# A two-layer decoder trunk on one core: turning the input of the next stage at the end of an FFN, and low halves of weights by an adding DMA

## The chip, the cores and the metric

The kernel runs on one core of one Trainium2 chip. The metric is the device time of one launch in microseconds (us); the time before is the median of three runs. TensorE (PE) multiplies, PEld is its weight load, VectorE (DVE) and ScalarE (ACT) work elementwise, GpSimd (POOL) here issues adding DMAs, and SyncE (SP) issues the plain DMAs. The profile comes from one further execution; times inside it count from its first instruction.

## What is computed

Two layers, each with three sub-layers on x, which is 512 tokens by 1024 features in float32:

```python
for l in range(DEPTH):
    h = rms_norm(x, gn[0])
    x = x + 0.5 * rms_norm(swiglu(h, w_ffn1_gate[l], w_ffn1_up[l], w_ffn1_down[l]), gn[1])
    h = rms_norm(x, gn[2])
    ...                                   # HGRN2 recurrence and windowed attention, gated, then w_out
    x = x + rms_norm(mixed @ w_out[l], gn[3])
    h = rms_norm(x, gn[4])
    x = x + 0.5 * rms_norm(swiglu(h, w_ffn2_gate[l], w_ffn2_up[l], w_ffn2_down[l]), gn[5])
```

`swiglu(h, g, u, d)` is `(silu(h @ g) * (h @ u)) @ d`, with an inner width of 2816. So there are four FFNs and two mixers, and each begins with a norm of the x that the one before it leaves.

## The kernel before

**Split products.** Every large matrix is multiplied in a reduced float type, float32r, and each operand is split into a high half (a cast) and a low half (the operand minus its high half). A product is three matmuls, `mm3` (line 408): high by high, then high by the other operand's low half, then low by high. PE runs its instructions in the order in which the code gives them (`manual_schedule`, line 52). The order on the other engines is the scheduler's, except for instructions passed to `pin`, which keep the order of the code among themselves.

**The stream of weights.** `Stream` (line 155) holds all weights in the order in which PE uses them, as units of 128x1024 elements. `load` (line 234) brings a unit into one of four buffers `w32` by a DMA on SP's queue; where a unit must be put together from four pieces it is four DMAs (line 240). A buffer is reused when all readers of the earlier unit are done. `split` (line 321) makes the halves `whi` and `wlo`, of which there are six each (`WS`); `ahead` (line 369) lets it run three units (`AHEAD`) before the unit that PE uses. ACT makes the high half by a cast (line 352). The low half depends on the unit's kind: kind "u" subtracts the high half from the weight on DVE (line 359); for the kinds "v", "a" and "d" ACT writes minus the weight into the float32r tile of the low half, which rounds it to minus the high half (line 356), and an adding DMA that POOL issues (line 357) adds the float32 weight to it. Either way the low half is first read by the second matmul of `mm3`.

**The end of an FFN.** `down` (line 688) multiplies by the last matrix; `y[t][h]` is the sum for token tile t (four of 128 tokens) and half h of the features (512 each). In an FFN (`fast`) 16 of the 22 blocks of the inner width go through seven products of a Strassen scheme (`quarters`, line 904). The last six blocks, three units per half h, are multiplied straight: those of h=0 first (`both`, line 729), those of h=1 last (`piece`, line 710). On PE the end is: product 5, the pieces of t=0 and t=1 with the three units of h=1, product 4 for t=2 and t=3, the pieces of t=2, then `pre.turn(0, ...)`, then the pieces of t=3, then the next stage's first products (`quad`, line 948).

**The norms there.** `half` (line 814) adds a sum to its Strassen part on DVE (line 820), squares it on ACT with a sum (`squares`, line 624, pinned) and multiplies by the gain on DVE (line 823). `post(t)` (line 836) takes the root (`root`, line 629: DVE, ACT's square root, pinned, and DVE's reciprocal) and adds the result to x (line 841). `norm(t)` (line 845) squares the new x, takes a root and scales it (line 852) into `xn[t]`, the next stage's normalized input with tokens on the partitions.

**The turn.** `Pre.turn` (line 599) turns `xn` to features on the partitions for half of the tokens (half 0: t=0 and 1). PE transposes four feature blocks at a time (line 124, from line 607), 16 transposes in all, into four PSUM banks; each bank is emptied into the high half by two ACT instructions (line 612, pinned) and into the low half by two on DVE (line 618). There are five banks of tag `acc` and three of tag `aux`. The second half (t=2 and 3) is turned by `rest` (line 867), which PE's order places a fixed count of work after the next stage has begun. The next stage's `quad` goes over the first half of the tokens with four units of weights, and then over the second half with the same units. While the first pass of `quad` runs, `ws.pinned` pins the casts of the weights; it is also set from product 6 until `half(1, 1)`.

Behind the last FFN there is no next stage, so nothing is turned. Behind a mixer (`fast` false) the turn stands at another place, which the change leaves as it was.

Of the kernel before, what the change touches and what calls it, by code (L numbers as in the profile page):

```python
# [7 lines left out]
F32 = mybir.dt.float32  # L8
F32R = mybir.dt.float32r
# [35 lines left out]
def trunk(ctx: ExitStack, tc: tile.TileContext, xin, wall, gains, lbT, hgain, sinks, c_dist, c_mask, c_ident, out):  # L45
# [109 lines left out]
    class Stream:  # L155
# [38 lines left out]
        def rows(self, kt, fast):  # L194

            u0 = self.wall

            def pieces(j, h):  # L200
                b = [(4 * h + i) * kt + 2 * j for i in range(4)]
                return [(slice(i * 2 * P, (i + 1) * 2 * P), wall[u0 + n // 8][:, n % 8 * P : (n % 8 + 2) * P]) for i, n in enumerate(b)]

            def unit(j, h):
                c = 2 * j * P
                self.src[self.n] = [(None, wall[u0 + 4 * h : u0 + 4 * h + 4, :, c : c + 2 * P].rearrange("u p c -> p u c"))] if kt == 8 else pieces(j, h)
                self.plain(1)

            lead = range(SEVEN // 2 if fast else 0, kt // 2)
            for j in lead:  # L210
                unit(j, 0)
            if fast:

                u, n = self.n, SEVEN // 4
                for q in range(n):
                    self.src[u + q] = pieces(q, 0)
                    self.src[u + n + q] = pieces(n + q, 0)
                self.side.append(([pieces(n + q, 1) for q in range(n)], [pieces(q, 1) for q in range(n)]))
                def product(k):
                    for q in range(n):  # L220
                        it = Item(k, u, 4)
                        it.q, it.n = q, n
                        self.items.append(it)

                for k in ORDER:
                    product(k)
                self.n += 2 * n
            for j in lead:
                unit(j, 1)
            if fast:  # L230
                product("p4")
            self.wall = u0 + kt
# [88 lines left out]
        def split(self):  # L321
            it = self.items[self.done]
            if it.kind[0] == "p":
                return self.quarter(it)
            u, last = it.u, it.kind in "uvd"
            self.load(u + (1 if it.kind in "uv" else 2))
            it.hi = sb.tile([P, D], F32R, tag="whi", name=nm("whi"), bufs=WS)
            it.lo = sb.tile([P, D], F32R, tag="wlo", name=nm("wlo"), bufs=WS)
            w, h = self.raw[u], (slice(0, D // 2), slice(D // 2, D))
            cols = (slice(0, D),)  # L330
            if it.kind == "u" and u == 0:
                cols = h
            if it.kind in "bcd":
                v = self.raw[u + 1]
            if it.kind == "b":

                self.t13 = sb.tile([P, D], F32, tag="tt", name=nm("tt"), bufs=2)
                pin(nc.vector.tensor_tensor(self.t13[:, h[0]], w[:, h[0]], v[:, h[0]], op=ALU.add))
                pin(nc.vector.tensor_tensor(self.t13[:, h[1]], v[:, h[0]], v[:, h[1]], op=ALU.add))
                w = self.t13  # L340
                self.product()
            elif it.kind == "c":

                t = sb.tile([P, D], F32, tag="tt", name=nm("tt"), bufs=2)
                pin(nc.vector.tensor_tensor(t[:, h[0]], self.t13[:, h[0]], v[:, h[1]], op=ALU.add))
                pin(nc.vector.tensor_tensor(t[:, h[1]], t[:, h[0]], w[:, h[1]], op=ALU.add))  # L346
                w = t
            elif it.kind == "d":
                w = v
                cols = h[1:]  # L350
            for c in cols:
                i = nc.scalar.copy(it.hi[:, c], w[:, c])  # L352
                if u < 3 or self.pinned or self.tight:
                    pin(i)
                if it.kind in "vad":
                    self.hold(nc.scalar.mul(it.lo[:, c], w[:, c], -1.0))  # L356
                    nc.gpsimd.dma_start(it.lo[:, c].bitcast(F32), w[:, c], accum_op=ALU.add)  # L357
                else:
                    self.hold(nc.vector.tensor_tensor(it.lo[:, c], w[:, c], it.hi[:, c].bitcast(F32), op=ALU.subtract))  # L359
            self.done += 1  # L360
            self.flight += 1
            if last:
                nu = u + (1 if it.kind in "uv" else 2)
                for i in range(u, nu):
                    self.raw.pop(i)
                    self.freed += 1
                self.load(self.freed + W32)
# [207 lines left out]
    class Pre(Quarters):  # L575
# [20 lines left out]
        def raw(self, half, i):  # L596
            return [cut(self.h[k + 4 * i], HALF[half]) for k in range(4)]

        def turn(self, half, get):

            c = HALF[half]
            for kp in range(KT // 2):
                p = get(kp)
                for i in range(2):
                    for t in range(2):
                        k = 2 * kp + i
                        transpose(p[:, (2 * i + t) * P : (2 * i + t + 1) * P], self.xn[2 * half + t][k // 4][:, k % 4 * P : (k % 4 + 1) * P])
                for i in range(2):
                    k = 2 * kp + i
                    if half == 0:  # L610
                        self.h.append((big(F32R), big(F32R)))
                    pin(nc.scalar.activation(
                        out=self.h[k][0][:, c], in_=p[:, i * 256 : (i + 1) * 256], func=AF.Copy,
                        scale=g_sb[:, self.l, self.n, k : k + 1],
                    ))
                for i in range(2):
                    k = 2 * kp + i
                    nc.vector.scalar_tensor_tensor(
                        self.h[k][1][:, c], p[:, i * 256 : (i + 1) * 256], g_sb[:, self.l, self.n, k : k + 1],
                        self.h[k][0][:, c].bitcast(F32), op0=ALU.mult, op1=ALU.subtract,  # L620
                    )
                self.have[half] += 2

    def squares(v, o):

# [62 lines left out]
    def down(src, kt, l, n, nxt, fast):  # L688
# [145 lines left out]
            left[0] -= 1  # L834

        def post(t):
            if not fast or t != 1:
                half(t, 1)
            rc = root(ss[t], D)
            for h in range(2):  # L840
# [34 lines left out]
        for t in range(TT):  # L875
# [5 lines left out]
            for j, b in zip(last, bs):  # L881
# [1 line left out]
                    piece(b, t, 1, j, i)  # L883
                    order.poll()
                ws.used(b)
                if pre and (t, j) == ((2, last[-1]) if fast else (3, last[TURN])):
                    pre.turn(0, lambda kp: acc() if kp < 3 else aux())
                    if not fast:
                        norm(2)
            if not fast or t > 1:  # L890
                post(t)
                after(t)
            elif t == 0:
                post(0)
            else:
                half(1, 1)
                ws.pinned = False
# [531 lines left out]
    for l in range(DEPTH):  # L1429
        for n in (0, 2, 4):  # L1430
            if n == 2:
                ws.plain(2 * H + 6 + 8 + LATE * 3 // 2)
                for _ in range(KT - LATE // 2):
                    ws.gates()
                ws.rows(KT, False)
            else:
                p = FIRST if l + n == 0 else 3
                ws.plain(min(2 * p, 8))
                ws.plain(max(2 * p - 8, 0), "v")
                ws.pairs(FT - p)  # L1440
                ws.rows(FT, True)
# [155 lines left out]
```

## Time and profile before

| | |
|---|---|
| median of 3 runs | 2089.57 us (2086.2 to 2092.58) |
| the profiled execution | 2090.36 us |
| its span, first to last instruction | 2088.6 us |
| PE busy in the span | 2071.2 us, 99% |
| PEld busy | 1862.1 us, 89% |
| DVE busy | 1645.3 us, 79% |
| ACT busy | 1242.3 us, 59% |
| POOL busy | 257.2 us, 12% |

The page of the profile lists busy times, the time in 40 slices, the DMA queues and the costliest groups. The view of waits says which instruction sat idle on its engine and which other instruction released it: "DVE rt L634 <- ACT rt L633: 11.2, 16, 0.8" says that line 634 on DVE waited for line 633 on ACT, 11.2 us in all, 16 times, 0.8 us at most. A row of the timeline is the start, the duration, engine, line, operation, output<-input, the shape and the count, and in brackets the idle time before it with its releaser. A matmul's duration there is its latency; the distance between two starts is what it costs PE.

### The profile page before, as it was taken

The page shows a single profiled execution, that of the slowest core. Times are in us where ns is not written, and L with a number is a line of the kernel's source. Part 1 is how long each engine was busy: PE and PEld are TensorE (multiplying, and loading weights), DVE is VectorE, ACT ScalarE, POOL GpSimd, SP SyncE. Part 2 cuts the span into 40 slices and gives each one's busy share as a digit, 9 for nine tenths or more (in the row PEclk, how much of TensorE's full clock was granted, in tenths as well). Part 3 has the DMA queues.
Part 4 walks back from the last instruction along what each step waited for, and adds up shares of the span by engine and source line. Part 5 has one row for each costly group of instructions (what it writes and reads, how often), then busy time and mean ns, then how long its engine had stood idle before and what let it go on. Part 6 is the DMA issues. An engine that isn't in the chain of part 4 may idle for free.

```text
span 2088.6 us, 36534 instructions
## 1 busy us (share of the span) xinstructions
PE 2071.2 (99%) x13561; PEld 1862.1 (89%) x13561; DVE 1645.3 (79%) x2921; ACT 1242.3 (59%) x2194; POOL 257.2 (12%) x306
## 2 busy tenths in 40 slices
PE   9999999999999999999999999999999999999998
PEld 7899988887898999998899999888778989999986
DVE  5887889766776778878988878987677758787888
ACT  6556686456354556558756566854653545665684
POOL 0111140000000011113101111300000000111140
PEclk9999999999999999999999999999999999999999
DMA  8587795312246368779737877943122552777694
GB/s 246 151 186 186 173 204 193 112 61 71 72 98 206 112 152 187 186 179 207 196 103 186 188 186 190 198 168 102 51 81 61 136 188 92 187 185 183 174 207 121
DMA packets 165074, 321.78 MB, mean 154 GB/s; under 512 B 18880, under 2 KB 84896, under 8 KB 164896
## 3 DMA queue, kind: packets, MB, share of 16 engines
q1 hardware_dynamic: 122416, 228.16, 32.8%
q0 software_dynamic: 42336, 91.24, 26.4%
q8 instruction: 106, 1.74, 0.3%
q14 instruction: 72, 0.59, 0.1%
q10 hardware_dynamic: 144, 0.05, 0.0%
HBM read 213.43 MB, written 14.73 MB: 109 GB/s over the span
## 4 chain that ended last, share of the span: by engine, by line
PE 87%; ACT 4%; DVE 3%; DMA 3%; issue 2%; SPq 1%; DVEq 0%; ACTq 0%
PE acc L114 64%; PE aux L114 21%; DMA w<-wall 1%; PE aux L124 1%; DVE s L260 1%; ACT whi L285 1%; ACT s L438 1%; DMA s<-wall 1%; PE acc L124 1%; ACT s L439 1%; DVE wlo L293 1%; SPq L240 1%; DVE s L429 0%; DMA s<-xin 0%; ACT s L428 0%
## 5 line engine op out<-in xcount | busy, mean ns | idle before, releaser
L114 PE MATMUL acc<-s,whi 128*128 128x256 f32 (+1 forms) x4976 | 1053.3, 309 | 1.4 <-ACT whi L352 0.8
L114 PEld LDWEIGHTS acc<-s,whi 128*128 128x128 f32 x4976 | 809.7, 191 | 49.2 <-issue 3.2
L114 PE MATMUL acc<-s,wlo 128*128 128x256 f32 (+1 forms) x2488 | 765.2, 308 | 0.1
L114 PEld LDWEIGHTS acc<-s,wlo 128*128 128x128 f32 x2488 | 475.6, 191 | 23.3 <-DVE wlo L359 0.4
L114 PE MATMUL acc<-whi,s 128*128 128x512 f32 x1360 | 441.7, 393 | 0.0
L352 ACT CAST whi<-w 128x1024 fp32r<-128x1024 f32 (+1 forms) x309 | 287.1, 933 | 168.0 <-PE acc L114 90.8
L352 ACT CAST whi<-tt 128x1024 fp32r<-128x1024 f32 x160 | 167.6, 1048 | 255.8 <-DVE tt L346 195.1
L114 PEld LDWEIGHTS acc<-whi,s 128*128 128x128 f32 x1360 | 255.3, 188 | 57.5 <-ACT whi L352 1.6
L359 DVE TENSOR_TENSOR wlo<-tt,whi 128x1024 fp32r<-128x1024 f32 x160 | 196.1, 1226 | 137.0 <-ACT whi L352 134.7
L357 POOL DMA_DIRECT2D wlo<-w x166 | 143.3, 863 | 1200.1 <-DVE wlo L359 504.6
L114 PE MATMUL acc<-wlo,s 128*128 128x512 f32 x680 | 265.1, 390 | 0.0
L114 PE MATMUL aux<-s,whi 128*128 128x256 f32 (+1 forms) x1296 | 239.2, 285 | 0.0
L359 DVE TENSOR_TENSOR wlo<-w,whi 128x1024 fp32r<-128x1024 f32 (+1 forms) x143 | 172.0, 1214 | 81.6 <-ACT whi L352 79.7
L114 PEld LDWEIGHTS aux<-s,whi 128*128 128x128 f32 x1296 | 202.7, 192 | 1.1 <-issue 0.5
L114 PE MATMUL aux<-s,wlo 128*128 128x256 f32 (+1 forms) x648 | 184.3, 284 | 0.0
L114 PEld LDWEIGHTS acc<-wlo,s 128*128 128x128 f32 x680 | 127.8, 188 | 25.4 <-DVE wlo L293 0.4
L114 PE MATMUL aux<-whi,s 128*128 128x512 f32 x432 | 143.7, 390 | 0.0
L356 ACT ACTIVATE wlo<-w 128x1024 fp32r<-128x1024 f32 (+1 forms) x166 | 140.7, 848 | 0.0
L440 POOL DMA_DIRECT2D s<-s x128 | 111.2, 945 | 218.5 <-ACT s L428 97.3
L114 PEld LDWEIGHTS aux<-s,wlo 128*128 128x128 f32 x648 | 124.4, 192 | 0.3
L293 DVE TENSOR_TENSOR wlo<-s,whi 128x512 fp32r<-128x512 f32 x160 | 102.7, 685 | 9.9 <-ACT whi L285 9.9
L428 ACT CAST s<-s 128x512 fp32r<-128x512 f32 (+1 forms) x140 | 70.7, 547 | 44.8 <-DVE s L487 41.4
(181 smaller groups left out, 2481.7 us busy)
## 6 DMA issues: line engine op xcount, KB each, us to landing
w<-wall SPq DMA_DIRECT2D x267, 512.0 KB, 3.8
wlo<-w POOLq DMA_DIRECT2D x86, 512.0 KB, 5.3
w<-wall SPq DMA_DIRECT2D x224, 128.0 KB, 3.5
wlo<-w POOLq DMA_DIRECT2D x80, 256.0 KB, 3.4
s<-wall SPq DMA_DIRECT2D x128, 128.0 KB, 3.9
s<-s POOLq DMA_DIRECT2D x64, 256.0 KB, 4.4
x_d<-s SPq DMA_DIRECT2D x48, 256.0 KB, 2.0
s<-x_d SPq DMA_DIRECT2D x48, 256.0 KB, 4.7
```

The costliest lines, as they stand in the source:

```text
L114: nc.tensor.matmul(o, lhsT, rhs, start=start, stop=stop)
L124: nc.tensor.transpose(o, src, ident)
L240: nc.sync.dma_start(w.rearrange("p (m c) -> p m c", m=4) if c is None else w[:, c], a)
L260: pin(nc.vector.tensor_tensor(o[c], x[c], y[c], op=op))
L285: i = nc.scalar.copy(it.hi[:, h[c]], w[c])
L293: pin(nc.vector.tensor_tensor(it.lo[:, h[c]], w[c], it.hi[:, h[c]].bitcast(F32), op=ALU.subtract))
L352: i = nc.scalar.copy(it.hi[:, c], w[:, c])
L356: self.hold(nc.scalar.mul(it.lo[:, c], w[:, c], -1.0))
L357: nc.gpsimd.dma_start(it.lo[:, c].bitcast(F32), w[:, c], accum_op=ALU.add)
L359: self.hold(nc.vector.tensor_tensor(it.lo[:, c], w[:, c], it.hi[:, c].bitcast(F32), op=ALU.subtract))
L428: (hold or ws.hold)(nc.scalar.copy(hi, src))
L440: nc.gpsimd.dma_start(lo.bitcast(F32), src, accum_op=ALU.add)
```

## The change

It has two parts.

**The turn.** `turn` gets an argument `later`, and the emptying of a bank moves into a method `leave`. Behind an FFN with a next stage, the 16 transposes stand at the same place of PE's order, but one bank is of tag `acc` and three of `aux` (before: three `acc` and one `aux`), and the emptying of the four banks is written between the steps of the norms: bank 0 between `half(2, 1)` and `post(2)`, bank 1 between `post(2)` and `norm(2)`, then, behind the pieces of t=3, bank 2 between `post(3)` and `norm(3)`, and bank 3 after `norm(3)`. Before, all four stood ahead of `half(2, 1)`.

**Low halves by an adding DMA.** Units of kind "u" become kind "v": the three units of h=1 at the end of each of the four FFNs (line 229), and the four units of the `quad` that follows an FFN (both mixers, and the first FFN of layer 1). The ACT instruction of line 356 is pinned where the cast ahead of it is pinned by `ws.pinned`; before, only where `ws.tight` was set.

```diff
--- before.py
+++ after.py
@@ -201,10 +201,10 @@
                 b = [(4 * h + i) * kt + 2 * j for i in range(4)]
                 return [(slice(i * 2 * P, (i + 1) * 2 * P), wall[u0 + n // 8][:, n % 8 * P : (n % 8 + 2) * P]) for i, n in enumerate(b)]
 
-            def unit(j, h):
+            def unit(j, h, kind="u"):
                 c = 2 * j * P
                 self.src[self.n] = [(None, wall[u0 + 4 * h : u0 + 4 * h + 4, :, c : c + 2 * P].rearrange("u p c -> p u c"))] if kt == 8 else pieces(j, h)
-                self.plain(1)
+                self.plain(1, kind)
 
             lead = range(SEVEN // 2 if fast else 0, kt // 2)
             for j in lead:
@@ -226,7 +226,7 @@
                     product(k)
                 self.n += 2 * n
             for j in lead:
-                unit(j, 1)
+                unit(j, 1, "v" if fast else "u")
             if fast:
                 product("p4")
             self.wall = u0 + kt
@@ -353,7 +353,9 @@
                 if u < 3 or self.pinned or self.tight:
                     pin(i)
                 if it.kind in "vad":
-                    self.hold(nc.scalar.mul(it.lo[:, c], w[:, c], -1.0))
+                    i = nc.scalar.mul(it.lo[:, c], w[:, c], -1.0)
+                    if self.pinned or self.tight:
+                        pin(i)
                     nc.gpsimd.dma_start(it.lo[:, c].bitcast(F32), w[:, c], accum_op=ALU.add)
                 else:
                     self.hold(nc.vector.tensor_tensor(it.lo[:, c], w[:, c], it.hi[:, c].bitcast(F32), op=ALU.subtract))
@@ -596,30 +598,38 @@
         def raw(self, half, i):
             return [cut(self.h[k + 4 * i], HALF[half]) for k in range(4)]
 
-        def turn(self, half, get):
-
-            c = HALF[half]
+        def turn(self, half, get, later=False):
+
+            outs = []
             for kp in range(KT // 2):
                 p = get(kp)
                 for i in range(2):
                     for t in range(2):
                         k = 2 * kp + i
                         transpose(p[:, (2 * i + t) * P : (2 * i + t + 1) * P], self.xn[2 * half + t][k // 4][:, k % 4 * P : (k % 4 + 1) * P])
-                for i in range(2):
-                    k = 2 * kp + i
-                    if half == 0:
-                        self.h.append((big(F32R), big(F32R)))
-                    pin(nc.scalar.activation(
-                        out=self.h[k][0][:, c], in_=p[:, i * 256 : (i + 1) * 256], func=AF.Copy,
-                        scale=g_sb[:, self.l, self.n, k : k + 1],
-                    ))
-                for i in range(2):
-                    k = 2 * kp + i
-                    nc.vector.scalar_tensor_tensor(
-                        self.h[k][1][:, c], p[:, i * 256 : (i + 1) * 256], g_sb[:, self.l, self.n, k : k + 1],
-                        self.h[k][0][:, c].bitcast(F32), op0=ALU.mult, op1=ALU.subtract,
-                    )
-                self.have[half] += 2
+                outs.append(lambda kp=kp, p=p: self.leave(half, kp, p))
+                if not later:
+                    outs.pop()()
+            return outs
+
+        def leave(self, half, kp, p):
+
+            c = HALF[half]
+            for i in range(2):
+                k = 2 * kp + i
+                if half == 0:
+                    self.h.append((big(F32R), big(F32R)))
+                pin(nc.scalar.activation(
+                    out=self.h[k][0][:, c], in_=p[:, i * 256 : (i + 1) * 256], func=AF.Copy,
+                    scale=g_sb[:, self.l, self.n, k : k + 1],
+                ))
+            for i in range(2):
+                k = 2 * kp + i
+                nc.vector.scalar_tensor_tensor(
+                    self.h[k][1][:, c], p[:, i * 256 : (i + 1) * 256], g_sb[:, self.l, self.n, k : k + 1],
+                    self.h[k][0][:, c].bitcast(F32), op0=ALU.mult, op1=ALU.subtract,
+                )
+            self.have[half] += 2
 
     def squares(v, o):
 
@@ -834,7 +844,7 @@
             left[0] -= 1
 
         def post(t):
-            if not fast or t != 1:
+            if not fast or t > 1 and not pre:
                 half(t, 1)
             rc = root(ss[t], D)
             for h in range(2):
@@ -883,14 +893,27 @@
                     piece(b, t, 1, j, i)
                     order.poll()
                 ws.used(b)
-                if pre and (t, j) == ((2, last[-1]) if fast else (3, last[TURN])):
+                if pre and not fast and (t, j) == (3, last[TURN]):
                     pre.turn(0, lambda kp: acc() if kp < 3 else aux())
-                    if not fast:
-                        norm(2)
-            if not fast or t > 1:
+                    norm(2)
+            if pre and fast and t == 2:
+                outs = pre.turn(0, lambda kp: aux() if kp else acc(), True)
+                half(2, 1)
+                outs[0]()
+                post(2)
+                outs[1]()
+                norm(2)
+            elif pre and fast and t == 3:
+                half(3, 1)
+                post(3)
+                outs[2]()
+                norm(3)
+                outs[3]()
+            elif not fast or t > 1:
                 post(t)
                 after(t)
             elif t == 0:
+                half(0, 1)
                 post(0)
             else:
                 half(1, 1)
@@ -1429,13 +1452,15 @@
     for l in range(DEPTH):
         for n in (0, 2, 4):
             if n == 2:
-                ws.plain(2 * H + 6 + 8 + LATE * 3 // 2)
+                ws.plain(4, "v")
+                ws.plain(2 * H + 2 + 8 + LATE * 3 // 2)
                 for _ in range(KT - LATE // 2):
                     ws.gates()
                 ws.rows(KT, False)
             else:
                 p = FIRST if l + n == 0 else 3
-                ws.plain(min(2 * p, 8))
+                ws.plain(4, "v" if l and not n else "u")
+                ws.plain(min(2 * p, 8) - 4)
                 ws.plain(max(2 * p - 8, 0), "v")
                 ws.pairs(FT - p)
                 ws.rows(FT, True)
```

## The prediction, written before the result was known

> **What bounds the kernel now.** I read the page first, then PE's waits, then the timeline around each wait.
>
> ```profile
> PE 2071.2 (99%) x13561; PEld 1862.1 (89%) x13561; DVE 1645.3 (79%) x2921; ACT 1242.3 (59%) x2194; POOL 257.2 (12%) x306
> ```
>
> PE is busy for 99% of the span, so what can be won is what PE still waits for, and any new wait of PE is paid in full. PE's waits, the longest first (total, times, longest):
>
> ```profile
> PE acc L124 <- DVE s L852: 5.7, 3, 1.9
> PE acc L124 <- DVE s L841: 2.6, 1, 2.6
> PE aux L114 <- DVE wlo L359: 2.5, 4, 1.1
> ```
>
> Two of the three lie where the change works. The first is the second turn behind the three FFNs that have a next stage: PE's transposes wait for `xn[3]`, the last result of `norm(3)`. The third comes four times, once in each FFN: the first low half of the units for h=1 at t=0. The second is at the very end of the kernel, where nothing is turned, and stays. So the change can win at most 5.7 + 2.5 = 8.2 us.
>
> **The turn.** PE behind the first FFN (the next stage's first product, then the second turn), then ACT and DVE there:
>
> ```profile
> 353.16 0.40 PE L114 MATMUL acc<-s,whi 128*128 128x256 f32 x2
> ```
>
> ```profile
> 362.04 0.27 PE L124 MATMUL acc<-ident,s 128*128 128x128 f32 x1
> 364.20 0.55 PE L124 MATMUL acc<-ident,s 128*128 128x128 f32 x3 [1.90 <-DVE s L852]
> ```
>
> ```profile
> 349.56 0.82 ACT L612 ACTIVATE s<-acc,g_sb 128x256 fp32r<-128x256 f32 x2
> ```
>
> ```profile
> 353.03 0.85 ACT L612 ACTIVATE s<-aux,g_sb 128x256 fp32r<-128x256 f32 x2
> 353.74 0.66 ACT L627 ACTIVATE s<-s 128x512 f32<-128x512 f32 x1
> ```
>
> ```profile
> 348.81 0.68 DVE L820 TENSOR_TENSOR s<-acc,s 128x512 f32<-128x512 f32 x1
> ```
>
> ```profile
> 353.65 0.68 DVE L820 TENSOR_TENSOR s<-acc,s 128x512 f32<-128x512 f32 x1
> ```
>
> ```profile
> 360.93 1.42 DVE L841 SCALAR_TENSOR_TENSOR s<-s,rt,s 128x512 f32<-128x512 f32 x2
> ```
>
> ```profile
> 363.66 0.88 DVE L852 TENSOR_SCALAR s<-s,rt 128x512 f32<-128x512 f32 x2
> ```
>
> `half(2, 1)` has its sum at 348.81 + 0.68 = 349.5, but its square runs at 353.74: it is pinned behind the eight evictions of line 612. Everything of t=2 and then of t=3 is late by these 4.2 us. The change lets two evictions (0.82) stand between that square and the root, and two more (0.85) ahead of `norm(2)`. I follow the longer of the two remaining chains, that of t=3, from its sum at 353.65, which PE sets: the sum 0.68, a square with its read 0.9, a root with its reciprocal and handovers 0.6, so line 841 starts at about 355.8 instead of 360.93. From line 841 to line 852 it is 363.66 - 360.93 = 2.7; bank 2's two evictions may come between, 0.85. That puts line 852 at 359.4 and its first result at 359.9, 2.1 before PE comes for it at 362.04. The norm of t=2 is done by then: it no longer waits for four banks. Bank 1 must be empty when the next stage reads its features: it starts at 353.16, and each bank feeds 24 matmuls of 256 columns, at half of the 0.227 us that 512 take (below) 2.7 us, so bank 1 is wanted at 355.9, banks 2 and 3 at 358.6 and 361.3; by the chain above they are empty at about 353, 357 and 360, in time by 3, 2 and 1. PE's order, the place of the second turn and the count of transposes stay as they were, and the third `aux` bank, which held `y[3][0]`, is read at 348.2 by line 820, earlier still once DVE has less to do. I put the turn's win at the whole 5.7 us, three times 1.9. If the cover fails (the margin of 2.1 is used up), at most the 5.7 stay.
>
> **Low halves at the end of the FFN.** These three units per FFN come just in time already. ACT's casts of all three behind the first FFN (I call the FFNs A, B, C, D) and of the first unit in the others:
>
> ```profile
> 317.00 1.05 ACT L352 CAST whi<-w 128x1024 fp32r<-128x1024 f32 x1 [0.99 <-DMA w<-wall]
> 319.00 1.05 ACT L352 CAST whi<-w 128x1024 fp32r<-128x1024 f32 x1 [0.95 <-DMA w<-wall]
> 321.64 1.05 ACT L352 CAST whi<-w 128x1024 fp32r<-128x1024 f32 x1 [1.60 <-DMA w<-wall]
> ```
>
> ```profile
> 1007.28 1.06 ACT L352 CAST whi<-w 128x1024 fp32r<-128x1024 f32 x1 [0.58 <-DMA w<-wall]
> ```
>
> ```profile
> 1351.86 1.06 ACT L352 CAST whi<-w 128x1024 fp32r<-128x1024 f32 x1 [0.80 <-issue]
> ```
>
> ```profile
> 2042.53 1.05 ACT L352 CAST whi<-w 128x1024 fp32r<-128x1024 f32 x1 [0.65 <-DMA w<-wall]
> ```
>
> The casts wait for the weights themselves, so they don't move earlier. PE's wait in the four places, and DVE's subtractions in A:
>
> ```profile
> 324.07 0.50 PE L114 MATMUL aux<-wlo,s 128*128 128x512 f32 x1 [0.58 <-DVE wlo L359]
> ```
>
> ```profile
> 1014.77 0.50 PE L114 MATMUL aux<-wlo,s 128*128 128x512 f32 x1 [0.34 <-DVE wlo L359]
> ```
>
> ```profile
> 1359.12 0.50 PE L114 MATMUL aux<-wlo,s 128*128 128x512 f32 x1 [1.12 <-DVE wlo L359]
> ```
>
> ```profile
> 2049.94 0.50 PE L114 MATMUL aux<-wlo,s 128*128 128x512 f32 x1 [0.47 <-DVE wlo L359]
> ```
>
> ```profile
> 322.80 3.49 DVE L359 TENSOR_TENSOR wlo<-w,whi 128x1024 fp32r<-128x1024 f32 x3
> ```
>
> Without the wait PE wants the first low half at 323.49 (A), 1014.43 (B), 1358.00 (C) and 2049.47 (D). DVE was busy until 322.80, so the cast of 317.00 lay there for 4.7 us. The change takes 3.5 us off DVE in each FFN and ends this wait; in its place comes the path over ACT, POOL and the DMA. One such path as the kernel has it elsewhere, and the sizes and times to landing of all of them:
>
> ```profile
> 1063.95 1.05 ACT L352 CAST whi<-w 128x1024 fp32r<-128x1024 f32 x1 [5.05 <-PE acc L114]
> ```
>
> ```profile
> 1066.26 0.86 POOL L357 DMA_DIRECT2D wlo<-w  x1 [62.28 <-ACT wlo L356]
> ```
>
> ```profile
> DMA to landing us min/median/max: 4.6/4.6/4.6
> ```
>
> ```profile
> wlo<-w POOLq DMA_DIRECT2D x86, 512.0 KB, 5.3
> ```
>
> ```profile
> wlo<-w POOLq DMA_DIRECT2D x80, 256.0 KB, 3.4
> ```
>
> From the cast's start to POOL's issue it is 1066.26 - 1063.95 = 2.3 us, and 4.6 more to landing with nothing alongside. With loads alongside it is longer; two windows from an add's issue to its landing show it (first the plain queue's packets, MB and share of the window, then the add with its time to landing), then the share of the DMA engines in the four microseconds from the issue in A and in D, before the change, as the last number but one:
>
> ```profile
> q1 hardware_dynamic: 571, 0.59, 31.6%
> ```
>
> ```profile
> wlo<-w POOLq DMA_DIRECT2D x1, 512.0 KB, 6.0
> ```
>
> ```profile
> q1 hardware_dynamic: 403, 0.98, 43.5%
> ```
>
> ```profile
> wlo<-w POOLq DMA_DIRECT2D x1, 512.0 KB, 8.0
> ```
>
> ```profile
> 319.30:323.30 4.00, 4.00 (x19) 3.15 (x17) 4.00 (x7) 2.40 (x4) 0.00 (x0) 1.00 0.71 223
> ```
>
> ```profile
> 2044.83:2048.83 4.00, 4.00 (x19) 3.33 (x18) 4.00 (x8) 3.13 (x5) 0.00 (x0) 1.00 0.87 276
> ```
>
> The plain queue had 31.6% of 6.0 = 1.9 us of work beside the first add and 43.5% of 8.0 = 3.5 us beside the second. In A there are 0.71 x 4 = 2.8 us of loads (the third unit's weights, and x for the norms), so I take 4.6 + (8.0 - 4.6) / 3.5 x 2.8 = 7.3 as the upper and 4.6 + (6.0 - 4.6) / 1.9 x 2.8 = 6.7 as the lower estimate, and use 6.7 for A and, as an estimate from its likeness, for B and C. D has 0.87 x 4 = 3.5: 8.0. The first low half then lands at cast + 2.3 + this:
>
> A 317.00 + 2.3 + 6.7 = 326.0, 2.5 late. B 1016.3, 1.9 late. C 1360.9, 2.9 late. D 2052.8, 3.3 late. Sum 10.6.
>
> The next two adds follow in the same queue. Two adds of 512 KB issued 1.9 us apart:
>
> ```profile
> L357 POOL DMA_DIRECT2D wlo<-w x2: 865/934/1004, 32.9 to 34.8; - x2
> ```
>
> ```profile
> DMA to landing us min/median/max: 7.0/7.3/7.6
> ```
>
> They land at 39.9 and 42.4, 2.5 apart. PE uses up a unit at t=0 in six matmuls of 0.227 (18 whole ones in 4 us, row above), 1.36 us. So the second and the third unit are each 2.5 - 1.36 = 1.14 later still: 2.3 per FFN, 9.1 in all. New waits 10.6 + 9.1 = 19.7; the old 2.5 goes. **This part costs 17.2 us.** From t=1 on all six halves are there.
>
> What else moves: the buffers `w32` come free at the add's landing instead of after the subtraction, so SP's next load, and five loads of x queued behind it, go out some 2 us later; the casts of the next units wait for a free `whi` until 337.78 in A, and PE is later too: nothing. ACT gets 1.0 us for each of 24 units, in gaps: its 59% leaves them.
>
> **Low halves in the next stage's first pass.** Four units, three times. DVE loses four subtractions of 1.2 us around the turn, which is spare already once the turn waits for nothing. Behind A the first and the fourth are cast here:
>
> ```profile
> 337.78 1.06 ACT L352 CAST whi<-w 128x1024 fp32r<-128x1024 f32 x1 [0.46 <-PE aux L114]
> ```
>
> ```profile
> 350.64 1.05 ACT L352 CAST whi<-w 128x1024 fp32r<-128x1024 f32 x1 [0.26 <-PE acc L114]
> ```
>
> The first three have 9 us and more until they are used, one after another 2.7 apart from 353.16 on. The fourth waits for a free tile and is wanted at 353.16 + 8.2 = 361.3; 350.64 + 2.3 + 8.0 is 360.9 even with loads alongside, so nothing, and up to 2 us each, 6 in all, if ACT's pinned evictions push the negation back by that much. Below nothing there is no room: PE doesn't wait there now.
>
> **The sum.** -5.7 + 17.2 = +11.5 on the profiled execution's 2090.36: 2101.9. That execution lies 0.8 above the median of the runs, so 2101.1; I say 2101.
>
> The Trainium skill ("DMA: Bandwidth & Descriptors", section on the anatomy of one DMA on the SWDGE path) fits such a transfer's time as 2.0 us plus bytes over 436e3; for 512 KB that would be 3.2 us, an estimate by that page, with which the first low halves are in time and the sum is about -6. The add above took 4.6 with nothing alongside, so the trace doesn't agree.
>
> **The rivals.**
>
> *The adds land in time* (not slower). If an add took 3.4 us, as the 256 KB ones do, A's first low half would land at 322.7, ahead of 323.49, and its third at 327.3 against 326.2: at most 1.1 late. With 0 to 4.4 us for the four together instead of 2.5, and the turn's 5.7, that is 2081 to 2086. It decides at 4.2, 4.9, 3.8 and 4.6 us to landing (wanted time less issue in A to D); for it speaks that DVE's backlog is real, against it that the add that ran alone, at 4.6, is at that border and loads run alongside. 10%.
>
> *The adds run as if alone.* At 4.6 to landing the first are 0.4, 0, 0.8 and 0 late, with 9.1 for the queue 10.3: -2.5 - 5.7 + 10.3 = +2.1, 2092. At the median of 5.3 it is +4.6, 2094. 24%.
>
> *The turn keeps a wait* (the change doesn't do what it says): the adds as forecast, and the 5.7 not won or a late fourth unit of up to 6 in its place: 2107. 8%.
>
> *The forecast*, adds slowed by loads: 2096 to 2105 (8.0 us to landing in all four gives 14.5 for the first halves, -5.7 - 2.5 + 14.5 + 9.1 = +15.4). 58%.
>
> **How the numbers follow.** Eight in ten: the forecast, the adds alone and the turn that keeps a wait hold 90%; the range is 2089 to 2110 (the adds at 8.0 and the turn's 5.7 not won give 2110) and leaves out the adds in time and the edges. About 0.3%, 6.3 us, is what a measurement of this kernel can tell from no change. Faster by more needs the adds in time nearly everywhere: 0.08. Within it are the adds alone and the rest of those in time: 0.27. Slower: 0.65.
>
> **What would show it.** Right: PE's wait for line 852 is gone; "PE aux L114 <- DVE wlo L359" is replaced by a wait for the DMA `wlo<-w`, with three steps in each FFN, the first 2 to 3 us, the next about 1. The squares of `half(2, 1)` come straight after its sum. Wrong: adds of 512 KB at the end of the FFN that land within 4.5 us, or in less than 2.5 us of each other; line 852 still late at the second turn; waits in the next stage's first pass.

## The result, and the profile after

The changed kernel takes 2112.44 us (median of 6 runs, 2108.54 to 2114.1) where the kernel before, beside it on the same chip, took 2090.69. The ratio is 1.0101, with a 95% interval of 1.0085 to 1.0117: slower by 21 us, in the forecast direction but 2 us beyond the end of the forecast range. The profiled execution took 2113.47 us, its span is 2111.7. Engines first, as for the kernel before:

```profile
PE 2083.1 (99%) x13561; PEld 1868.5 (88%) x13561; DVE 1621.3 (77%) x2897; ACT 1263.1 (60%) x2218; POOL 277.2 (13%) x330
```

PE is "busy" for 99% again, of a span 23 us longer, with the same 13561 matmuls. The waits of PE after (total, times, longest):

```profile
PE aux L114 <- DMA wlo<-w: 19.5, 12, 5.0
PE acc L124 <- DVE s L851: 2.6, 1, 2.6
PE aux L114 <- DVE eps_t L137: 1.1, 1, 1.1
PE acc L114 <- ACT whi L352: 0.8, 1, 0.8
```

Line 852 (862 in the changed file) is gone from the list. In place of the 2.5 us for VectorE's low half stand 19.5 us for the DMA, twelve times, three per FFN. That is nearly the 19.7 us of the prediction, but by luck: the four first waits are 3.23, 3.23, 4.96 and 3.18 us, 14.6 where 10.6 was forecast, and the eight others 4.9 where 9.1 was forecast, because PE, itself slowed, came late to them. And the total is far off all the same: the list of waits doesn't hold the rest. It is in how fast PE works between these waits. PE at the end of FFN A, the units of h=1 at t=0 (start, duration, wait in brackets):

```profile
326.43 0.79 PE L114 MATMUL aux<-wlo,s 128*128 128x512 f32 x1 [3.23 <-DMA wlo<-w]
327.02 1.05 PE L114 MATMUL aux<-whi,s 128*128 128x512 f32 x2
...
330.73 0.79 PE L114 MATMUL aux<-wlo,s 128*128 128x512 f32 x1 [1.37 <-DMA wlo<-w]
...
333.91 0.80 PE L114 MATMUL aux<-wlo,s 128*128 128x512 f32 x1 [0.26 <-DMA wlo<-w]
...
336.47 0.63 PE L114 MATMUL aux<-whi,s 128*128 128x512 f32 x2
```

Two matmuls take 1.05 us from 327.02 on and 0.63 from 336.47 on. The same stretch by windows (PE, PEld, DVE, ACT, POOL busy; granted clock; DMA share; GB/s):

```profile
318.68:322.09 3.41, 3.41 (x16) 2.83 (x16) 3.41 (x7) 3.31 (x5) 1.72 (x2) 1.00 0.97 256
322.09:325.51 3.42, 1.11 (x5) 0.57 (x4) 3.42 (x7) 3.39 (x6) 0.86 (x1) 1.00 1.04 254
325.51:328.92 3.41, 2.49 (x6) 1.82 (x6) 3.02 (x6) 3.28 (x8) 0.00 (x0) 0.50 1.10 283
328.92:332.33 3.41, 2.04 (x6) 1.32 (x5) 0.00 (x0) 0.00 (x0) 0.00 (x0) 0.50 1.05 237
332.33:335.75 3.42, 3.16 (x8) 2.01 (x7) 0.00 (x0) 0.00 (x0) 0.00 (x0) 0.50 1.03 394
335.75:339.16 3.41, 3.41 (x16) 2.81 (x15) 2.95 (x5) 0.72 (x2) 0.00 (x0) 1.00 0.86 350
```

Two things are to be seen. The granted clock is 0.50 for three windows after one in which PE had 1.11 us of work; at the four FFNs' ends together it is 0.50 for 41 us. And the DMA engines are busy without a gap, a share of 0.97 to 1.10, for as long as the adds are under way. What they carried: SP's issues before and after, in the same place (an "x5" is five loads in a row).

```profile
318.06 1.35 SPq L727 DMA_DIRECT2D s<-x_d  x3
324.05 0.33 SPq L243 DMA_DIRECT2D w<-wall  x1
324.48 2.55 SPq L727 DMA_DIRECT2D s<-x_d  x5
```

```profile
318.35 5.34 SPq L737 DMA_DIRECT2D s<-x_d  x7
326.44 0.33 SPq L243 DMA_DIRECT2D w<-wall  x1
326.87 1.41 SPq L737 DMA_DIRECT2D s<-x_d  x1
```

Before, the next load of weights stood between the third and the fourth load of x and held five of them back until its buffer was free. After, that load stands behind the seventh, so seven of the eight loads of x go out beside the first adds. In FFN B and C it is the same; behind D no weights follow, and the eight loads of x go out in one row before and after. From issue to landing the three adds took, in FFN A, B, C and D:

```profile
DMA to landing us min/median/max: 7.3/9.6/10.7
DMA to landing us min/median/max: 8.6/9.3/9.8
DMA to landing us min/median/max: 8.0/9.5/11.2
DMA to landing us min/median/max: 8.6/9.1/9.6
```

I add up the stage "pieces of t=0 and t=1" (36 matmuls from the first `aux<-whi` to the next product): before 9.04, 8.79, 9.59 and 8.96 us in A to D, together 36.4; after 17.30, 16.80, 20.09 and 15.77, together 70.0. That is +33.6, of which 17.0 are waits (19.5 less 2.5) and 16.6 are matmuls at half clock. The turns and what lies around them give some 10 back (8.1 of it between the first turn's start and the second's end, in three places): +23.1 between the two profiled executions.

### The profile page after: what moved, and what is told of

The parts are those of the page before. It is cut to its first block, busy times and chain, and to the rows that moved or that the text cites. A ratio compares the mean times of both kernels' runs of the same rounds, so it can differ in the third digit from the quotient of the medians.

```text
span 2111.7 us, 36595 instructions
## 1 busy us (share of the span) xinstructions
PE 2083.1 (99%) x13561; PEld 1868.5 (88%) x13561; DVE 1621.3 (77%) x2897; ACT 1263.1 (60%) x2218; POOL 277.2 (13%) x330
## 5 line engine op out<-in xcount | busy, mean ns | idle before, releaser
L114 PEld LDWEIGHTS acc<-s,wlo 128*128 128x128 f32 x2488 | 475.1, 191 | 23.1 <-DVE wlo L361 0.4
L359 POOL DMA_DIRECT2D wlo<-w x190 | 163.6, 861 | 1292.1 <-DVE wlo L361 502.1
L361 DVE TENSOR_TENSOR wlo<-w,whi 128x1024 fp32r<-128x1024 f32 (+1 forms) x119 | 143.3, 1213 | 81.4 <-ACT whi L352 79.6
L356 ACT ACTIVATE wlo<-w 128x1024 fp32r<-128x1024 f32 (+1 forms) x190 | 165.7, 873 | 0.0
L114 PE MATMUL aux<-whi,s 128*128 128x512 f32 x432 | 153.2, 414 | 0.0
L293 DVE TENSOR_TENSOR wlo<-s,whi 128x512 fp32r<-128x512 f32 x160 | 102.6, 685 | 12.5 <-ACT whi L285 12.4
L114 PE MATMUL aux<-wlo,s 128*128 128x512 f32 x216 | 91.7, 425 | 19.5 <-DMA wlo<-w 19.5
```

The lines of the kernel that those rows point to most:

```text
L114: nc.tensor.matmul(o, lhsT, rhs, start=start, stop=stop)
L293: pin(nc.vector.tensor_tensor(it.lo[:, h[c]], w[c], it.hi[:, h[c]].bitcast(F32), op=ALU.subtract))
L356: i = nc.scalar.mul(it.lo[:, c], w[:, c], -1.0)
```

## The experiments

The theory after the result has three parts: the adds cost what they cost with little beside them (the prediction's 17); the loads of x that now run beside them make them land later; and PE's waits bring half clock behind them. The rivals: the adds are slow by their own queue whatever runs beside them, and half clock alone is the overrun.

**The turn without any new add.** Each `"v"` of the change is a `"u"` again:

```
-                unit(j, 1, "v" if fast else "u")
+                unit(j, 1)
...
-                ws.plain(4, "v")
+                ws.plain(4, "u")
...
-                ws.plain(4, "v" if l and not n else "u")
+                ws.plain(4, "u")
```

> The changed kernel with every low half subtracted by VectorE again, so that only the new order of the turn is left. My theory now: the turn is worth more than the 5.7 us of the prediction, because in the changed kernel the distance between the two turns fell and the 3.41 us of half clock behind the old wait at 1056 are gone too: 8 to 10 us less than before, 2080 to 2083. The prediction's figure would give 2085. Rival: the turn only gained in the changed kernel because the adding DMAs took four subtractions from VectorE there; then the wait for the root's scaling (L862) comes back in part and the gain is under 4 us, 2087 or more. The waits for a low half before t=0 are again four steps of VectorE with about 2.5 us in all.

Measured: 2084.44 us, ratio 0.9962 [0.9948, 0.9975], so 7.9 us less than before; the interval, 5 to 11, holds the prediction's 5.7 as well as my 8 to 10. By the trace the three turns won 1.7, 2.1 and 1.7 us (from the first turn's start to the second's end, 18.68 to 16.96 in A): the prediction's 5.7 nearly to the digit. Of the rest of the first expectation the trace shows one piece: the half clock behind FFN B's old wait is gone, and the 50 matmuls behind that turn take 5.98 us instead of 7.12. That the turn is worth 8 to 10 us isn't shown. One small wait is left in this kernel, at the first turn:

```profile
350.21 0.66 PE L124 MATMUL aux<-ident,s 128*128 128x128 f32 x4 [0.17 <-DVE s L830]
```

**The turn and the adds of the next stage's first pass.** Only the first of the three edits above:

> The changed kernel with VectorE's subtraction for the last three units of each FFN only; the new turn and the adding DMAs of the next stage's first pass are kept. My theory, as in the prediction: these adds cost nothing, so within 1.5 us of the turn alone, 2079 to 2084. Rival one: they cost up to 6 us (late fourth unit), 2087. Rival two: they relieve VectorE at the turn and gain 2 us or more, under 2079.

Measured: 2081.13 us, ratio 0.9950 [0.9938, 0.9962], 10.4 us less than before and the fastest kernel here. The step from the turn alone, 2.5 us, lies inside the intervals, but the trace has its place: the first turn's matmuls run through without the wait above, and the two turns start 14.47 us apart, not 15.32, behind each of three FFNs (3 x 0.85 = 2.6).

```profile
348.17 0.60 PE L124 MATMUL acc<-ident,s 128*128 128x128 f32 x4
348.61 1.47 PE L124 MATMUL aux<-ident,s 128*128 128x128 f32 x12
```

VectorE starts to empty the third `aux` bank (line 830) at 345.49 here and at 349.47 with the turn alone, 4 us later. So by the trace the four subtractions that the adds take over were not spare there, and rival two of the expectation has the right size, though its figure (under 2079) was missed and the step in the runs is not clear of noise.

**The adds at the FFN's end alone.** The kernel before with these lines:

```
-            def unit(j, h):
+            def unit(j, h, kind="u"):
...
-                self.plain(1)
+                self.plain(1, kind)
...
-                unit(j, 1)
+                unit(j, 1, "v" if fast else "u")
...
-                    self.hold(nc.scalar.mul(it.lo[:, c], w[:, c], -1.0))
+                    i = nc.scalar.mul(it.lo[:, c], w[:, c], -1.0)
+                    if self.pinned or self.tight:
+                        pin(i)
```

> The kernel before with the adding DMAs for the last three units of each FFN alone; old turn, low halves of the next stage's first pass by VectorE. My theory: the whole loss is here, some 31 to 35 us, 2121 to 2126: 17 of waits for the DMA and the rest of half clock behind them. The prediction's figure is 17.2 us, 2108. Rival: the adds of the next stage's first pass have part of the loss; then less than 28 us, under 2118.

Measured: 2114.38 us, ratio 1.0110 [1.0096, 1.0124]: +23 us. That is less than my 31 and more than the prediction's 17, in the range of the rival; but the rival's reason is not the one, since the pass's adds won time in the run above. The loss is here, and it is 9 us smaller than the step from the turn and the pass (0.9950) to the whole change (1.0101), which is 32 us. Its waits say half of why (line 854 is the old line 852):

```profile
PE aux L114 <- DMA wlo<-w: 22.8, 11, 4.7
PE acc L124 <- DVE s L854: 1.3, 3, 0.4
```

The old turn's wait is 1.3 us instead of 5.7 without any change of the turn. VectorE has three subtractions less and PE comes later, so the norms are nearly in time. The other half is at the FFNs' ends: the four stages take 66.5 us in all, 3.5 less than in the changed kernel, and the clock there is at 0.50 for 20 us, not 41. The gain of the new turn and the loss of the adds don't add up: beside these adds the turn is worth little.

**Zeros in the waits.** PE is kept busy ahead of the three units at t=0:

```
             for j, b in zip(last, bs):
+                if fast and t == 0:
+                    for _ in range(14 if j == last[0] else 8):
+                        nc.tensor.matmul(y[0][1], zt[0], halves(b[2], 0), start=False, stop=False)
                 for i in range(2):
                     piece(b, t, 1, j, i)
...
+        zt.append(const([P, P], "zt", F32R))
+        nc.scalar.mul(zt[0], ones, 0.0)
```

> The changed kernel with 14, 8 and 8 useless matmuls of a zero matrix, added to one bank of the sum, ahead of the three units at t=0, so that PE is busy while the adds land; the sum is unchanged, the work is added and of no use. If idling is what halves the clock behind these waits, the windows at 0.5 there are gone. Theory A, the third landing sets the end of the pieces anyway and half clock mostly lies beside the waits: 4 to 6 us less than the changed kernel, 2106 to 2109. Theory B, half clock is paid in full on top of the waits: 11 to 16 us less, 2096 to 2101. Null: the clock is halved for another reason, the windows stay, and the time is that of the changed kernel or up to 8 us more.

Measured: 2108.85 us, ratio 1.0086 [1.0072, 1.0100], some 3 us less than the changed kernel. The windows of half clock at the FFNs' ends are gone (the mean clock is 0.999, one window is left in the last microseconds of the kernel), and 120 extra matmuls are hidden:

```profile
322.68 3.41 PE L894 MATMUL aux<-whi,zt 128*128 128x512 f32 x14
...
327.98 0.50 PE L114 MATMUL aux<-wlo,s 128*128 128x512 f32 x1 [1.66 <-DMA wlo<-w]
...
334.88 0.50 PE L114 MATMUL aux<-wlo,s 128*128 128x512 f32 x1
...
340.25 0.39 PE L114 MATMUL acc<-whi,s 128*128 128x512 f32 x1
```

```profile
330.00:334.00 4.00, 4.00 (x19) 3.24 (x18) 0.85 (x2) 0.00 (x0) 0.00 (x0) 1.00 1.02 279
```

So idling does halve the clock here, and theory A holds: the 16.6 us of half clock lie mostly beside waits that would otherwise be longer. Here too the third low half lands at 334.84, and 24 matmuls of 0.227 us follow it (5.4 us) to the stage's end at 340.25. Full clock moves only those of the 24 that were slow. The zeros themselves don't set the end: PE comes to the third low half at most 0.33 us after its landing in all four FFNs. From that landing to the stage's end it is 5.4 to 5.6 us here and 6.24, 6.48, 7.57 and 5.70 in the changed kernel, 4.1 more in all, which is the size of the measured step.

**x behind the adds.** The loads for tile 0 stay, the other six wait for the third low half:

```
-            for t in range(TT):
+            fetch_x(range(1 if fast else TT))
+
+        def fetch_x(ts, b=None):
+            for t in ts:
                 for h in range(2):
                     xt[t][h] = big()
+                    if b:
+                        nc.gpsimd.tensor_copy(xt[t][h][:, :1], b[3][:, :1].bitcast(F32))
                     nc.sync.dma_start(xt[t][h], x_d[t, h])
...
         bs = [ws.next(8, TT) for _ in last]
+        if fast:
+            fetch_x(range(1, TT), bs[-1])
```

> The changed kernel with the loads of x for token tiles 1 to 3 (six of 256 KB) made to wait, by a copied column, for the low half of the third unit; those for tile 0 go out as before. Theory A, the loads of x that now run beside the adds slow them: from the first add's issue to the third landing it takes 10 to 12 us instead of 15, the waits for the DMA at t=0 fall to 5 to 10 us in all, and the time is 10 to 17 us less than that of the changed kernel, 2096 to 2103. Theory B, the adds are slow in their own queue: first issue to third landing stays at 14 us or more, and the time within 3 us of the changed kernel, 2109 to 2116. A later x can cost up to 4 us at t=1 in either.

Measured: 2100.61 us, ratio 1.0045 [1.0030, 1.0060], 11.7 us less than the changed kernel. The three adds of FFN A to D from issue to landing:

```profile
DMA to landing us min/median/max: 6.0/6.4/8.4
DMA to landing us min/median/max: 7.0/7.5/7.6
DMA to landing us min/median/max: 5.6/6.1/8.5
DMA to landing us min/median/max: 6.6/6.8/7.2
```

From the first issue to the third landing it is 12.4, 12.8, 12.5 and 11.6 us instead of 14.8, 15.3, 15.2 and 15.2. Theory A holds; only the waits (15.7 us, expected 5 to 10) are longer than I said, probably because PE now comes to them at full clock more often (0.50 for 10 us at the FFNs' ends, not 41). Why the adds took 12 and not 10: the buffers that the first adds free let the next weights out beside the third. The second add lands 2.4 to 2.5 us behind the first in all four, the third another 3.9, 3.0, 4.5 and 2.5; the last is FFN D, behind which there are no next weights to load. What the adds and the plain loads took of the DMA engines from 319 to 332.1 (queue, packets, MB, share):

```profile
q0 software_dynamic: 432, 1.57, 66.8%
q1 hardware_dynamic: 756, 1.51, 34.8%
```

Together 101.6%: there is no room. From the first issue to the third landing in FFN A the adds took 54.1% of 14.84 us in the changed kernel and 70.7% of 12.37 us here, 8.0 and 8.7 us of all the engines' time, nearly the same; the plain loads took 7.4 us (2.40 MB) there and 3.9 us (1.28 MB) here. So what made the adds land later was the loads beside them. By the shares from 319 to 332.1 the adds moved 1.57 MB in 8.8 us of all the engines' time, 180 GB/s, and the plain loads 1.51 MB in 4.6 us, 330 GB/s.

**Both.** x behind the adds, and six matmuls of zeros ahead of each of the three units:

> The changed kernel with the later loads of x as in the run that puts them behind the adds, and six useless matmuls of zeros ahead of each of the three units at t=0. If half clock and the loads alongside are two causes that add up, it is another 2 to 5 us less than that run, and what is left over the version without adds at the FFN's end is the adds alone: 8 to 14 us. If only one cause is real, it is equal to the better of the two single runs within 2 us.

Measured: 2096.38 us, ratio 1.0028 [1.0018, 1.0039]. The step from x alone is 3.5 us, as that from the changed kernel to the zeros alone was 3.1; the loads of x are 11.7 without the zeros and 12.1 with them. So the two causes add up. Each step of half clock alone lies inside its intervals; that it has the same sign and size twice, with the windows at 0.5 gone from the FFNs' ends both times, is what speaks for it. By the traces the four stages are 5.0 us shorter with the zeros alone (70.0 to 65.0) and 1.8 with x behind as well (56.2 to 54.4), so the size of 3 is a rough one. What is left over the kernel with turn and pass (0.9950) is 16.3 us, 13 to 20 by the intervals: somewhat above my 8 to 14.

**One add of three.** Of the change only the third unit:

```
-                unit(j, 1, "v" if fast else "u")
+                unit(j, 1, "v" if fast and j == lead[-1] else "u")
```

> The changed kernel with an adding DMA for the last of the three units at the end of each FFN alone; the first two are subtracted by VectorE. Theory A: the first subtraction frees the buffer of the next weights early, which puts a load of weights ahead of five loads of x, the add has little beside it and lands 5 to 6 us after its issue, 1 to 3 us late per FFN, so 2 to 10 us over the version with none, 2083 to 2091, and no half clock behind it. Theory B, each add costs the same third of the loss: some 2092 to 2094 and a window of half clock in most FFNs.

Measured: 2106.71 us, ratio 1.0076 [1.0059, 1.0093]: both expectations fail. Over the kernel with turn and pass, one add costs 26 us where three cost 32. In FFN A, its time from issue to landing, and a window:

```profile
DMA to landing us min/median/max: 8.4/8.4/8.4
```

```profile
330.00:334.00 4.00, 1.75 (x4) 1.46 (x5) 0.91 (x2) 0.00 (x0) 0.00 (x0) 0.56 1.05 360
```

My step that it would have "little beside it" was wrong: VectorE's subtraction frees the weights' buffer at 323.80, in the same moment in which the add goes out (323.84), and that load and five of x run beside it. It lands at 332.21, 1.7 us ahead of the third add of the changed kernel. The stage's end hangs on the last landing; how early the first two low halves come is worth little.

**POOL in VectorE's place.** The turn and the pass as above, the three units at the FFN's end subtracted on POOL:

```
-                unit(j, 1, "v" if fast else "u")
+                unit(j, 1, "w" if fast else "u")
...
+                elif it.kind == "w":
+                    nc.gpsimd.tensor_tensor(it.lo[:, c], w[:, c], it.hi[:, c].bitcast(F32), op=ALU.subtract)
```

> The turn and the adds of the next stage's first pass as in the changed kernel, and the three units at the end of each FFN subtracted on POOL, which is idle there, instead of VectorE or an adding DMA. No trace here shows a subtraction on POOL, so its duration d is what this run measures. From the first cast's end to the third unit's use there are some 7.2 us: with d up to 2.4 us nothing is late, the waits for VectorE's low halves go, and the time is 2 to 4 us under the version without it, 2077 to 2079. With d = 3.5 it is 3.3 late per FFN and 2091 or so, with d = 5 some 2108.

Measured: 2096.43 us, ratio 1.0029 [1.0019, 1.0039], some 16 more than without it and above the line that its duration gives: d is 2.4 to 3.0 us and the low halves cost PE 2.9 us in three waits. The loss is in another place:

```profile
PE acc L114 <- DVE wlo L293: 10.2, 3, 5.2
PE aux L114 <- POOL wlo L361: 2.9, 3, 1.1
```

```profile
1007.35 2.39 POOL L361 TENSOR_TENSOR wlo<-w,whi 128x1024 fp32r<-128x1024 f32 x1 [4.13 <-ACT whi L352]
1010.04 5.24 POOL L361 TENSOR_TENSOR wlo<-w,whi 128x1024 fp32r<-128x1024 f32 x2 [0.29 <-ACT whi L352]
```

```profile
1006.72 0.69 DVE L433 TENSOR_TENSOR s<-s,s 128x512 fp32r<-128x512 f32 x1
1007.32 0.69 DVE L947 TENSOR_TENSOR s<-acc,s 128x512 f32<-128x512 f32 x1
1007.92 2.37 DVE L433 TENSOR_TENSOR s<-s,s 128x512 fp32r<-128x512 f32 x1
1010.21 5.62 DVE L293 TENSOR_TENSOR wlo<-s,whi 128x512 fp32r<-128x512 f32 x2
```

While POOL subtracts, VectorE's sums of two SBUF tiles (differences among them) take 2.4 to 2.9 us each here instead of 0.69, and PE waits for their results in line 293. The clock is at 0.50 about two of these waits (3.41 us in FFN B, 6.83 in D), which can cost up to 5 us more. The sum with a PSUM operand (`s<-acc,s`), which starts as POOL does, keeps its 0.69. The Trainium skill ("SBUF — State Buffer", section "SBUF: two separate sides") says that VectorE with two SBUF inputs and a GpSimd operation that reads SBUF take one port pair in turns, each for its whole instruction. The trace agrees: each such sum lasts about as long as the subtraction beside it.

## Why the prediction was too low

**The turn** was right. It said 5.7; the trace has 1.7, 2.1 and 1.7, together 5.5. The squares came where it said, line 852 no longer ended a wait, and the first result of `norm(3)` was there 2.1 us before PE came for it, the margin that it had worked out. That this margin fits to the digit is in part luck: from the sum of t=3 (361.12) to line 851 (364.08) it took 0.8 us longer than forecast and from there to line 862 0.7 less, and with the turn alone the margin is 1.4. VectorE's two results of line 862 (0.49 us the first), and PE's transposes of the second turn, of the changed kernel:

```profile
366.97 0.88 DVE L862 TENSOR_SCALAR s<-s,rt 128x512 f32<-128x512 f32 x2
```

```profile
369.55 0.60 PE L124 MATMUL acc<-ident,s 128*128 128x128 f32 x4
```

**The adds of the next stage's first pass** were put at nothing, with four subtractions of VectorE "spare already". They were not: the trace has 0.85 us less between the two turns behind each of three FFNs, and the runs 2.5 us, which lies inside their intervals.

**The adds at the FFN's end** were put at 17.2 and measure 32 us (0.9950 to 1.0101). This is the step that failed: the term of 17.2 us was too small, and what the adds do to SP's loads was put at nothing. It failed in two places.

- "SP's next load, and five loads of x queued behind it, go out some 2 us later": the load of weights did (326.44 in A, not 324.05), but four of the five loads of x went out ahead of it. The order of SP's issues wasn't the one of before, and these loads ran beside the adds. The term took 6.7 and 8.0 us to the first landing and 2.5 between landings; measured 7.4, 8.6, 8.0 and 8.7, and 3.2 to 4.3. With x behind the adds it is 6.0, 7.5, 5.6 and 6.6, and 2.4 to 2.5 for the second: with only the loads of tile 0 beside them the durations are near the forecast ones, within 1.1 us in A to C and 1.4 in D. The price of the rest is some 12 us (11.7 and 12.1 in the two pairs).
- "Any new wait of PE is paid in full": it is paid with more than its length where half clock follows it. The row that shows it stood in the trace of before, behind the wait of 1.88 us at FFN B's turn:

```profile
1052.60:1056.01 3.41, 1.53 (x14) 1.30 (x13) 2.42 (x6) 3.38 (x8) 0.00 (x0) 1.00 0.41 154
1056.01:1059.42 3.41, 3.41 (x18) 3.41 (x17) 3.41 (x8) 2.89 (x8) 0.00 (x0) 0.50 0.56 168
```

I read the mean clock there and not the windows. The price on top is only some 3 us, since most of the slow matmuls stood ahead of a landing that PE had to wait for anyway; behind the last landings they took 4.1 us.

What the adds cost without either, 16.3 us (13 to 20), is close to the prediction's 17.2. That is agreement in the sum and not in each part: in that run the first adds take 5.8 to 7.2 us to land (forecast 6.7 and 8.0), and the third land 3.0 to 4.6 us behind the second (forecast 2.5). The account in parts of the whole: turn -0.38%, pass -0.12%, adds as forecast +0.78%, loads of x +0.58%, half clock +0.15%, together +1.01%, 21 us. These are steps along one chain of kernels; in another order they differ, as the adds alone on the kernel before (+23 us) show.

The prediction asked what the adds do to SP's order only as a delay, never as another order; and even in the order of before, five loads of x would have run beside the second and the third add, which it counted with none. How much of the 12 us each of these two has isn't settled, since no run here varies the order alone. In FFN D, where the order stayed, the stage grew by 6.8 us, and in the other three by 8.0 to 10.5. Why the order differs is open too, as the diff doesn't touch those lines; but the runs show with what it goes. In FFN A it is the new one in the three kernels that have adds for all three units and issue x freely (the changed one, the adds alone, the zeros), and the old one with the turn alone, turn and pass, the third add only, and POOL. The kernel that wins is the change without its adds at the FFN's end: 2081.13 us, 0.9950 of the time before.

## What to carry to other kernels

Take the adding DMA for work whose result is wanted much later, as in the next stage's first pass; where a low half is wanted within 7 us, as at these FFNs' ends, VectorE's 1.2 us is the shorter way even at the end of a queue, and one late transfer cost nearly as much as three (26 and 32 us), because the last landing sets the end. Ask of a DMA what else will be on the engines in the order of issue that the changed program will have, not the one of before, and count shares: in these stages they were at 100%, and with six loads of x taken out the third add landed 2.5 to 3.6 us sooner after the first one's issue. Where PE's wait is counted, look at the granted clock in the windows behind it; the list of waits came out within 0.2 us here, by luck, and the time was wrong by 11.

## What the runs showed of the hardware

- PE's clock falls to 0.50 in steps of 3.41 us behind windows in which PE had little to do, and such a window need not be idle throughout: 1.53 us of work in 3.41 (before, at 1052.60) and 1.11 in 3.42 (after, at 322.09) were followed by half clock (the windows are cut at the clock's own steps). Zeros on PE in the waits kept it at 1.00. The Trainium skill ("TensorE: Matmul & The Clock Gate", Part 1) describes a free-running window of 3413 ns and half rate after an idle one. The length agrees; these two rows say that a window needn't be idle. Counted on in such steps through the ten traces, without their last 10 us, 17 windows at full clock with 1.40 us of PE work or less were all followed by half clock, and those with 1.55 or more by full clock; of the two between, the one of 1.53 above was followed by half clock, and one of 1.52 behind FFN C of the kernel before (1397.34) by full. So here the border lies near 1.5 us of 3.41.
- An adding DMA of 512 KB takes the DMA engines nearly twice as long for a byte as a plain load: 180 and 330 GB/s by the shares above. It is as slow alone: in the kernel before, from 1066.2 to 1071, an add took 57.3% of 4.8 us for 0.52 MB, which is 190 GB/s.
- A subtraction of 128x1024 on POOL took 2.4 to 3.0 us, twice VectorE's 1.2, and stopped VectorE's own sums of SBUF tiles for as long.
